# Another order of the instructions up to the first gate and up products, and seven products without use on TensorE in the opening

## The chip, the cores and the metric

The kernel runs on one core of one Trainium2 chip. The metric is the time of one execution on the device in microseconds (us), the median of several runs. The profile is of one further execution. Engines are named as the profile names them: PE (TensorE), DVE (VectorE), ACT (ScalarE), POOL (GpSimd) and SP (SyncE, which here only issues DMAs).

## The reference, cut to what matters

One decoder layer on x of 512 rows by 1024 columns, in float32. In short:

```
h    = rms_norm(x, attn_pre_norm)
proj = h @ w_in                         # one projection for both head groups
A    = 4 heads of differential attention: softmax(q1 k1) - lam * softmax(q2 k2), times v, then rms_norm
B    = 8 heads in 2 groups: g0 * compressed branch + g1 * selected branch + g2 * window branch
x    = x + rms_norm(concat(A, B) @ w_out, attn_post_norm)
f    = (silu(h2 @ w_gate) * (h2 @ w_up)) @ w_down,   h2 = rms_norm(x, ffn_pre_norm)
out  = x + rms_norm(f, ffn_post_norm)
```

The compressed branch passes blocks of 32 keys and values through a small two-layer network (k_cmp_w1, v_cmp_w1 and the like). With 512 rows the selected branch and the window branch reach every earlier row.

## The kernel before, in words

Every operand of a large product is split into a high part (float32 rounded to the form that PE multiplies in one pass) and a low part (the rest); a product is then hi*hi + hi*lo + lo*hi, three matmuls. ACT makes the high parts, DVE (in places POOL) the low parts. Names ending in h and l, or beginning with whi and wlo, are these parts.

The first two thirds of the program's instructions are written as some thirty *streams*, Python generators that issue a few instructions and then yield. Each stream has a letter. `TABLE` is a string of 1543 letters: the program takes them one after another and advances the stream of that letter by one step. So the string fixes the order of the instructions on each engine, and the order on each engine is kept: an instruction whose operands aren't ready holds all behind it on that engine. SP issues its DMAs in the same way, one behind the other. What lies behind the first gate and up products (the feed-forward part, from the products `gw` at L1250 on) is written out and isn't in the table.

The streams that the text speaks of:

- `a` x_loads, `b` x_highs, `c` x_lows: load x transposed in eight parts, scale it and split it into xh and xl. `b` also issues three products `warm` without use, and squares the parts (xraw, in place); `c` adds the squares up.
- `d` constants: the masks and the identity.
- `e` row_factors (L365 on): sums the squares over the partitions on PE with eight small products into ssum, makes the factor rstd of each row on ACT and DVE, spreads it with four products rb, and multiplies the rotation tables (ckv, skv, cos, sin) with it on DVE.
- `S` weights: loads 512 KB parts of the weights into wraw (three buffers), and splits them (three buffers for whi, three for wlo).
- `P` projections (L432 on): the products of the input projection in the order C v1 q1 k1 cv n1 ck s g q0 k0 v0 n0. The first pair, C (tiles fm4 and fm5), is multiplied in the order of the list OPEN as the parts of x come in. cv and ck are the first layer of the small network (tile cmp), n1, s and so on are pairs of tiles fm. The tiles fm, v and cmp take turns in two buffers of PSUM.
- `R` evictions: reads the fm tiles (ACT copies fm4 and fm5 to craw), rotates them on DVE into rope, splits them and writes them to memory (kcvc, qk).
- `K` compression: reads kcvc back as cx and makes cst, the operand of cmp, on ACT and DVE.
- `Q` loads: reads the queries and keys back (qst, kst). `A` scores: products sc. `X`, `E`, `Y`: row maximum on DVE, exponential on ACT, scaling of the rows (for the heads N the first of four row blocks on ACT, the other three on POOL). `Z`, `H`, `L`: transposes tr on PE and their split into pth and ptl. `V`: products av. `O`, `J`: outputs and their split into oh and ol (with the products ms and rsb for the norm of the heads D).
- `G`, `T`: the compressed scores scc, and their transposes trc.
- `W`, `M`, `N`: the output weights and the products mixp, mix. `w` to `z`: the norms of the four row blocks, with the transposes trh. `F`: the first gate and up products gu.

The heads are taken in the order D2 D3 N4 N5 N6 N7 D0 D1 N0 N1 N2 N3. The products without use multiply xh with itself into a PSUM tile (warm_ps) that nothing reads; before, 20 of them on zeros stand ahead of everything, and three on xh behind the first two parts of x.

Of the kernel before, what the change touches and what calls it, by code (L numbers as in the profile page):

```python
# [17 lines left out]
P = 128  # L18
# [30 lines left out]
HEADS = "D2 D3 N4 N5 N6 N7 D0 D1 N0 N1 N2 N3"  # L49
WORDER = "2 3 6 7 0 1 F0 4 5 F1"  # L50
TABLE = (
    "aaabbcaabbaaPcbPbcbaPaPbaaPbabcPPPPaaccPcPbPbPPPbPPbPcbPPcPdPbdcdPbPPcPbcPSPbcPcPPPPcPPPPcedPPPSSSSeePeP"
    "ePPPPaaPdSeeeRePPeRRSSRRRPRPPPSRPRSRPRSPPPSRRPKPRPPPPRSRPPRPSPSSSaKKPPPPPPPRRSPPPPPSSPSRRRRSSPPPPPRRdRKK"
    "KSRRSKSdPKPKRRRPSPQSdSPSPSSPRSPSPPKSRKKKKKdSRPPSPKKRPdSRdKKPPSRRRSSSdSPPPKdRKKKKKKKPPQSPRRSSKRPSPPPSSPAA"
    "SXPSQEXRRPSRPASPPQRKKPRPPSPSSXXARSARQXPPSEAPXRPKPQKESXGSPRPEESPKSKRPRAdAXPRSSKXdXEKESPRGRRRRPAPPEXGPRRPE"
    "RYRPPPPPRYYYXGPRRPPRGRYPYEYYYPPGSGSPSPPQRPQGGGEZQZQPHPLASAQERXXZAEQHXXARGGSSSSRPEEPERXSYPPGEAXXEGPAPAGYA"
    "HLGXVPRYAELXVREPEXYPSAGEVPVXEOXOYPGXSREPAPERRYRYRPSJJXJYSTPTYZSRRYXTJRPATAPHXZPSLYREJEZPQPAYPRESRJHPSHLX"
    "SRRRRRPJXPAEYYVYPLXZZRPREAPWRXXHRRYJEHVLXPPEEYAZRVHVSRXPWOPQAPOYYPYYWLRSZLHPYWSVLAEYXZXHLZAXWXVPAVRHYXPL"
    "VZYARHYXLEPPPRWVZVHZLPEPTAHESXTRAPVEPEEYVEXWAQVZHYPLWERZPXWPLROHWLWAYEJOWJZWJVPPJYQHXWVYYXLPVXRRAXTVVWYQ"
    "QRWYYVVEEEVTVRZAOHZAEAOJXHLRXLZYEJYHRMZJQARJHEELVMYVVYQRLXVEXYZHYXMRXZAALEEYYQVVHXVZLMAQHLVUZVZYXEJHXYJX"  # L60
    "AHELXALMEZOAAZUHXYHOXXLLYAMYGYVYVZGEVYYYHVGVYGMXLEEUWWEGVXZHZGVGEVLQVHGMOZMQEGHOGMEALLJEJXXAGAVXGEQUEYEY"
    "AQXMGXEGAYVXXEGGWVVMOMEAMGUOWYWGATXAXTJTMYYYYXEMTAJJYEZXJUHZAHWYMMXEALJEWWXLZMYYYYYYYYQXMEZEAJEXHLVWVHZJ"
    "MAXHALEEWVEVLZXWOYYMZOHQAYYXXELHEXAVYVLWXYYYJJEVZEVAAHXJEJEZLVXVHXVZLAJVEEVZMXOAHMXOHLEYLYWJWZZAJXAVHHLE"
    "ELXXYVTTZVYHYYJVXVZAWYLXVAWYWWMMEYHEEZLMHZEHXMLVVTEJYTWLVYOMWZZHYMOLVVJYYYHYZJWVVHLYLVZHMWLVYYZZVVVHHLML"
    "OZOHZLHMVVLZWWWVZHVLHLVVWVVVWOWOMOJOMMJJMMMMJBBBBNBNNNBwwwwwNxNxxwxxwxxxwwwxwwWNwNNNNxWNxwNxxwxwwNxwwxxx"
    "xxwwwNxNxxNxNWWWWNNNyWWyNyNNzyyzFFyyzFyzyFFzzzzyyyFFyzyzyFzyWzzzzyWFyyzzyyFzzzyyyzFzzFz"
)
HP = 400
POOL_LO = "157"
# [48 lines left out]
def hybrid_block_kernel(  # L118
# [6 lines left out]
    act, dve, pool, pe, sp = nc.scalar, nc.vector, nc.gpsimd, nc.tensor, nc.sync  # L125
# [81 lines left out]
    def ps(tag, name, dt=F32):  # L207
        return PS.tile([P, SEQ], dt, tag=tag, name=name, bufs=PSB[tag])
# [6 lines left out]
    warm_ps = ps("av", "warm")  # L215
# [24 lines left out]
    act, dve, pool, pe, sp = (Written(e) for e in (act, dve, pool, pe, sp))  # L240
    xh, xl = [], []
# [121 lines left out]
    def row_factors():  # L363

        yield ["sums", "ident"]  # L365
        ssum = ps("tr", "ssum")[:, :NT]
        for i in range(NT):
            for j in range(2):
                pe.matmul(ssum[:, i:i + 1], obj["sq", j][:, i * P:(i + 1) * P], ones, start=(j == 0), stop=(j == 1))
        yield  # L370
        v, y, t = (cpool.tile([P, NT], F32, tag=f"rr{j}h", name="rr", bufs=2) for j in range(3))
        act.activation(y, ssum, AF.Ln, bias=eps, scale=1.0 / D_MODEL)
        act.activation(y, y, AF.Exp, scale=-0.5)
        yield
        dve.tensor_scalar(v, ssum, 1.0 / D_MODEL, EPS, OP.mult, OP.add)
        yield
        dve.tensor_tensor(t, y, y, OP.mult)
        dve.tensor_tensor(t, t, v, OP.mult)
        dve.tensor_scalar(t, t, -0.5, 1.5, OP.mult, OP.add)
        dve.tensor_tensor(rstd, y, t, OP.mult)  # L380
        yield
        rb = ps("tr", "rb")
        for i in range(NT):
            pe.matmul(rb[:, i * P:(i + 1) * P], rstd[:, i:i + 1].to_broadcast([P, P]), ident, start=True, stop=True)
        yield
        dve.tensor_scalar_mul(nrstd, rstd, -1.0)
        for j in (2, 3, 0, 1):
            yield ("rope", j)
            dve.tensor_tensor(rp[j], rb, rp[j], OP.mult)
            obj["table", j] = True  # L390
# [43 lines left out]
    def projections():  # L434
        for tok in PROJ.split():
            if tok == PROJ.split()[0]:
                ms, pts, done = [2 * PAIR[tok] + j for j in range(2)], [], [0, 0]
                for j, k, part in OPEN:
                    m = ms[j]
                    yield [("w", m)] + [[("xh", k)], [("xh", k), ("wl", m)], [("xl", k)]][part]  # L440
                    if not done[j]:
                        pts.append(ps("mm", f"fm{m}"))
                    w = obj["w", m][int(part == 1)]
                    pe.matmul(pts[j], w[:, k * P:(k + 1) * P], (xh, xh, xl)[part][k], start=(done[j] == 0),
                              stop=(done[j] == 3 * NK - 1))
                    done[j] += 1
                    if done[j] == 3 * NK:
                        del obj["w", m]
                        obj["fm", m] = pts[j]
            elif tok in PAIR:  # L450
                for m in (2 * PAIR[tok], 2 * PAIR[tok] + 1):
                    yield ("w", m)
                    hi, lo = obj.pop(("w", m))
                    pt = ps("mm", f"fm{m}")
                    for n in range(3 * NK):
                        if n and n % 4 == 0:
                            yield ("wl", m) if n == NK else None
                        w, x_ = ((hi, xh), (lo, xh), (hi, xl))[n // NK]
                        k = n % NK
                        pe.matmul(pt, w[:, k * P:(k + 1) * P], x_[k], start=(n == 0), stop=(n == 3 * NK - 1))  # L460
                    obj["fm", m] = pt
            elif tok[0] == "c":
                v = int(tok == "cv")
                for c in range(4):
                    yield [("w", tok, c), ("xs", v, c // 2)]
                    if not c:
                        hps = ps(CMPT, f"cmp{v}")
                    hl = obj.pop(("w", tok, c))
                    for l in range(4):
                        if l == 2:  # L470
                            yield
                        lh = 4 * c + l
                        t = obj["xs", v, lh // 8][:, lh % 8].rearrange("p s g n -> p (s g n)")
                        for wi, w in enumerate(hl):
                            pe.matmul(hps[:, :CMP_HIDDEN], t, w[:, l * 256:(l + 1) * 256],
                                      start=(lh == 0 and wi == 0), stop=(lh == NLH - 1 and wi == 1))
                obj["cmp", v] = hps
            else:
                cs, width = (2, 256) if tok[0] == "v" else (3, NVG)
                kc = NK // 2 if cs == 2 else 3  # L480
                ws = []
                for i in range(NT):
                    n = 0
                    for c in range(cs):
                        yield None if i else ("w", tok, c)
                        if not n:
                            pt = ps("mm", tok)[:, :width]
                        if not i:
                            ws.append(obj.pop(("w", tok, c)))
                        for j, (xx, wi) in enumerate(((xh, 0), (xl, 0), (xh, 1))):  # L490
                            if j == 2:
                                yield
                            for k in range(kc * c, min(kc * (c + 1), NK)):
                                w = ws[c][wi][:, (k - kc * c) * width:(k - kc * c + 1) * width]
                                pe.matmul(pt, xx[k][:, i * P:(i + 1) * P], w, start=(n == 0), stop=(n == 3 * NK - 1))
                                n += 1
                    obj[tok, i] = pt
# [668 lines left out]
    act, dve, pool, pe, sp = nc.scalar, nc.vector, nc.gpsimd, nc.tensor, nc.sync  # L1166
# [418 lines left out]
    for n, (r, c, t) in enumerate(banks):  # L1585
        i, bank = 2 * r + t, result[r][c][t]
# [7 lines left out]
        m, v, y, e, f, _, s0, s1 = (rows[i][:, j:j + 1] for j in range(8))  # L1594
# [106 lines left out]
```

## Time and profile before

| | us |
|---|---|
| median of 3 runs | 654.77 (654.54, 654.77, 657.61) |
| the profiled execution | 658.55 |
| its span in the profile | 656.5 |
| PE busy in the span | 636.7 (97%) |
| DVE busy | 545.3 (83%) |
| mean clock granted to TensorE | 0.991 |

The profile is a page and a trace that can be asked. Its timeline has a start, a duration, the engine, and for merged rows the number of instructions behind an x; brackets hold the idle time before and what ended it. The durations of matmuls overlap, so the pace of a run of them is the distance of the starts. A small float32 product (ssum, rb, ms, rsb) stands as two records. PEclk in a table of windows is the clock that TensorE was granted, 1.00 for the full one.

### The profile page before, as it was taken

The numbers are of one execution on the slowest core, as the hardware profiler recorded it, in microseconds if no ns is written. First come the engines' busy times: TensorE is split into PE (matmuls) and PEld (weight loads), VectorE is DVE, ScalarE is ACT, GpSimd is POOL, SyncE is SP. The second block draws the span as 40 slices with busy tenths as digits, with TensorE's granted clock in tenths as the row PEclk, the third lists the DMA queues.
The fourth block names the chain that finished last, engine by engine and source line by source line (L and its number), as shares of the span: only waits on it lengthen the run. The fifth ranks groups of instructions, "written<-read, shape, count | busy, mean of one in ns | idle before, by whom it ended". The sixth has DMA issues, their size and how long they took to land.

```text
span 656.5 us, 11115 instructions
## 1 busy us (share of the span) xinstructions
PE 636.7 (97%) x4081; PEld 569.9 (87%) x4081; DVE 545.3 (83%) x1050; ACT 390.6 (59%) x821; POOL 94.4 (14%) x100
## 2 busy tenths in 40 slices
PE   9899899999999999999999999999999999999995
PEld 5788789788988888887898999999999998888884
DVE  5757887789789798978999998888888639999866
ACT  7334554575567688955756655655655539675434
POOL 0000001112316236532200000000000101120023
PEclk9799999999999899999999999999999999999999
DMA  8354796715315423145414333223223547984543
GB/s 307 124 162 185 251 309 231 237 36 202 136 35 206 137 106 113 65 178 205 163 34 142 115 103 123 97 97 129 97 97 129 127 131 203 307 257 132 199 90 128
DMA packets 32902, 100.52 MB, mean 153 GB/s; under 512 B 4176, under 2 KB 5072, under 8 KB 31952
## 3 DMA queue, kind: packets, MB, share of 16 engines
q1 hardware_dynamic: 30544, 95.62, 41.8%
q0 software_dynamic: 2304, 4.20, 3.8%
q8 instruction: 32, 0.52, 0.3%
q14 instruction: 22, 0.18, 0.1%
HBM read 85.64 MB, written 12.06 MB: 149 GB/s over the span
## 4 chain that ended last, share of the span: by engine, by line
PE 77%; DVE 12%; DMA 4%; ACT 3%; issue 2%; SPq 0%; DVEq 0%; ACTq 0%
PE gw L1250 28%; PE acc L1461 17%; PE fm L230 9%; PE av L230 4%; PE v L230 4%; PE sc L230 3%; PE mix L230 3%; PE tr L230 3%; PE g L230 2%; DMA wraw<-in_wf 2%; PE scc L230 1%; DVE rr L230 1%; DMA qk<-rope 1%; DVE mixt L230 1%; PE mixp L230 1%
## 5 line engine op out<-in xcount | busy, mean ns | idle before, releaser
L230 POOL TENSOR_TENSOR p<-p,l 128x384 f32<-128x384 f32 (+3 forms) x60 | 54.5, 939 | 126.0 <-DVE l L230 101.3
L230 ACT ACTIVATE p<-p,nm 128x128 f32<-128x128 f32 (+1 forms) x96 | 53.2, 556 | 12.3 <-DVE nm L230 10.3
L230 DVE CUSTOM_DVE_ANT_0 p<-sc,mask_b 128x128 f32<-128x128 f32 (+1 forms) x96 | 44.6, 483 | 7.1 <-PE sc L230 5.5
L230 ACT ACTIVATE whi<-wraw 128x1024 fp32r<-128x1024 f32 (+2 forms) x34 | 34.9, 1034 | 24.3 <-issue 13.1
L230 DVE TENSOR_TENSOR wlo<-wraw,whi 128x1024 fp32r<-128x1024 f32 (+2 forms) x34 | 40.9, 1209 | 8.6 <-ACT whi L230 8.6
L230 ACT ACTIVATE pth<-tr 128x384 fp32r<-128x384 f32 (+1 forms) x60 | 30.7, 521 | 25.1 <-PE tr L230 22.6
L230 DVE TENSOR_TENSOR ptl<-tr,pth 128x384 fp32r<-128x384 f32 (+1 forms) x60 | 35.2, 595 | 10.4 <-ACT pth L230 10.2
L230 PE MATMUL sc<-kst,qst 128*128 128x128 f32 (+1 forms) x192 | 41.3, 331 | 2.2 <-DMA kst<-qk 1.5
L1396 POOL DMA_DIRECT2D dr<-in_wd x8 | 7.0, 880 | 235.8 <-DVE wu L1284 189.3
L230 PE MATMUL fm<-xh,whi 128*128 128x512 f32 x128 | 35.4, 403 | 0.5 <-ACT whi L230 0.5
L230 PE MATMUL fm<-xh,wlo 128*128 128x512 f32 x128 | 35.0, 401 | 0.0
L230 PE MATMUL fm<-xl,whi 128*128 128x512 f32 x128 | 33.7, 394 | 0.0
L230 PEld LDWEIGHTS sc<-kst,qst 128*128 128x128 f32 x192 | 28.8, 189 | 5.3 <-DVE vn L230 1.9
L230 PE MATMUL tr<-ident,p 128*128 128x128 f32 x200 | 31.4, 280 | 1.4 <-DVE ptl L230 1.3
L230 PE MATMUL mix<-ws,oh 128*128 128x512 f32 x84 | 29.6, 403 | 0.0
L230 PEld LDWEIGHTS tr<-ident,p 128*128 128x128 f32 x200 | 24.2, 144 | 5.6 <-DVE ptl L230 1.8
L230 PEld LDWEIGHTS fm<-xl,whi 128*128 128x128 f32 x128 | 24.2, 190 | 5.0
L230 PEld LDWEIGHTS fm<-xh,wlo 128*128 128x128 f32 x128 | 24.1, 192 | 4.9
L230 PEld LDWEIGHTS fm<-xh,whi 128*128 128x128 f32 x128 | 23.5, 192 | 5.0 <-ACT whi L230 1.0
L1461 PE MATMUL acc<-whi,ah 128*128 128x512 f32 x60 | 23.5, 392 | 0.0
L1461 PE MATMUL acc<-whi,al 128*128 128x512 f32 x60 | 23.5, 392 | 0.0
L1461 PE MATMUL acc<-wlo,ah 128*128 128x512 f32 x60 | 23.5, 392 | 0.0
(368 smaller groups left out, 1956.0 us busy)
## 6 DMA issues: line engine op xcount, KB each, us to landing
wraw<-in_wg SPq DMA_DIRECT2D x22, 512.0 KB, 3.3
dr<-in_wd SPq DMA_DIRECT2D x22, 512.0 KB, 4.5
wu<-in_wu SPq DMA_DIRECT2D x19, 512.0 KB, 3.2
wraw<-in_wf SPq DMA_DIRECT2D x16, 512.0 KB, 4.7
qk<-rope SPq DMA_DIRECT2D x7, 1024.0 KB, 4.9
qst<-qk SPq DMA_DIRECT2D x24, 256.0 KB, 2.7
kst<-qk SPq DMA_DIRECT2D x24, 256.0 KB, 4.1
wraw<-in_wo SPq DMA_DIRECT2D x8, 512.0 KB, 3.3
```

Of the source, the lines that this page charges most:

```text
L230: r = getattr(self.eng, name)(*a, **k)
L1250: m = pe.matmul(pt, ww[:, k * P:(k + 1) * P], hx[k], start=(start and n == 0), stop=(n == 11), skip_group_check=True)
L1396: pool.dma_start(t[:, H], wd[pair(p)[0]][:, L], accum_op=OP.add)
L1461: m = pe.matmul(pt, x, y, start=(start and n == 0), stop=(stop and n == 2), skip_group_check=True)
```

## The change

The string TABLE is another one of the same length: each letter occurs as often as before, in another order throughout. And two streams issue more products without use: row_factors two, behind the first of the eight products ssum, and projections five, behind the last product of C. The core of the diff (of the table one line of fifteen):

```
 TABLE = (
-    "aaabbcaabbaaPcbPbcbaPaPbaaPbabcPPPPaaccPcPbPbPPPbPPbPcbPPcPdPbdcdPbPPcPbcPSPbcPcPPPPcPPPPcedPPPSSSSeePeP"
...
+    "aaaabbbcPcPaPPcaabbPaPaPcbPPPbacPPacPbPPPaPPPPbbPPbcPSPPPbPcbaPPPPPPPPabbcdbbaPSSdabcccbPScccceePPPPSSeP"
...
@@ row_factors
                 pe.matmul(ssum[:, i:i + 1], obj["sq", j][:, i * P:(i + 1) * P], ones, start=(j == 0), stop=(j == 1))
+                if i == j == 0:
+                    for _ in range(2):
+                        pe.matmul(warm_ps, xh[0][:, :P], xh[0], start=True, stop=True)
@@ projections, behind the loop over OPEN
+                for _ in range(5):
+                    pe.matmul(warm_ps, xh[0][:, :P], xh[0], start=True, stop=True)
```

What the order of the instructions makes of it is shown at three places.

**First place: PE in the opening.** Before, from the last part but one of x on:

```order
L230 MATMUL fm4_148<-xh6_177,whi_133 128x512
L230 MATMUL ssum_249<-ones_85,xraw_127 128x1 x8
L230 MATMUL fm5_181<-xh6_177,whi_152 128x512
...
L230 MATMUL rb_283<-ident_78,rstd_87 128x128 x4
...
L230 MATMUL fm5_181<-xl7_220,whi_152 128x512
L230 MATMUL v1_306<-whi_267,xh0_131 128x256
```

The same stretch after:

```order
L230 MATMUL fm4_140<-xh6_198,whi_134 128x512
L230 MATMUL ssum_257<-ones_85,xraw_127 128x1
L230 MATMUL warm_100<-xh0_132 128x512 x2
L230 MATMUL ssum_257<-ones_85,xraw_127 128x1 x7
L230 MATMUL fm5_165<-xh6_198,whi_157 128x512
...
L230 MATMUL rb_286<-ident_78,rstd_87 128x128 x4
...
L230 MATMUL fm5_165<-xl7_244,whi_157 128x512
L230 MATMUL warm_100<-xh0_132 128x512 x5
L230 MATMUL v1_321<-whi_250,xh0_132 128x256
```

Two products stand between the first and the second ssum, five between the last product of C and the first of v1; five products fm stand between ssum and rb, and six behind rb, in both. The three products on xh that were ahead of fm4 stand behind its fourth product now, and on DVE the casts of the masks have moved from ahead of the row factors to behind the first row blocks of v1.

**Second place: DVE and SP around the second product cmp** (cmp0, of ck; it takes the PSUM buffer of fm14 and reads cst). DVE before, where wlo_745 is the low part of ck's second weight part:

```order
L230 SCALAR_TENSOR_TENSOR rope_764<-fm14_683,cos_122 128x512
L230 TENSOR_TENSOR cst_762<-cx_716,cst_762 128x8x2x31
L230 TENSOR_TENSOR cst_762<-pos_718,cst_762 128x8x2
L230 TENSOR_TENSOR cst_770<-cx_716,cst_770 128x8x2x31
L230 TENSOR_TENSOR wlo_745<-wraw_680,whi_744 128x1024
L230 SCALAR_TENSOR_TENSOR rope_764<-fm14_683,sin_123 128x512
```

DVE after, where the same low part is wlo_761:

```order
L230 SCALAR_TENSOR_TENSOR rope_777<-fm14_677,cos_122 128x512
L230 SCALAR_TENSOR_TENSOR rope_777<-fm14_677,sin_123 128x512
L230 TENSOR_TENSOR wlo_761<-wraw_675,whi_760 128x1024
L230 TENSOR_TENSOR cst_783<-cx_718,cst_783 128x8x2x31
L230 TENSOR_TENSOR cst_783<-pos_720,cst_783 128x8x2
```

fm14 is read to the end, and ck's second weight part split, ahead of the cst instructions and no longer behind them. SP before, where in_wf are the two weight parts of the pair s, the next that PE multiplies:

```order
L230 DMA qk4_735<-rope_603 128x2048
L230 DMA wraw_741<-in_kw1 128x1x1024
L230 DMA kst_782<-qk4_735 64x1024 x2
L230 DMA wraw_792<-in_wf 128x1024
L230 DMA wraw_817<-in_wf 128x1024
```

SP after:

```order
L230 DMA wraw_756<-in_kw1 128x1x1024
L230 DMA qk4_775<-rope_584 128x2048
L230 DMA wraw_787<-in_wf 128x1024
L230 DMA kst_799<-qk4_775 64x1024 x2
L230 DMA wraw_813<-in_wf 128x1024
```

The first part of s is asked for ahead of the two reads kst, which wait for the write qk4 to land, and no longer behind them. On PE the first six products sc, which stood inside cmp0, are behind it.

**Third place: PE at the first scores of head N4** (kst_1248 before, kst_1249 after). Before:

```order
L230 MATMUL sc_1289<-kst_1219,qst_1211 128x512 x2
L230 MATMUL sc_1302<-kst_1248,qst_1242 128x128 x2
L230 MATMUL sc_1302<-kst_1248,qst_1242 128x256 x2
L230 MATMUL fm0_1214<-xh4_167,wlo_1199 128x512
...
L230 MATMUL fm1_1342<-xh3_160,whi_1310 128x512
```

After:

```order
L230 MATMUL sc_1294<-kst_1230,qst_1226 128x512 x2
L230 MATMUL fm0_1253<-xl0_142,whi_1214 128x512
...
L230 MATMUL fm0_1253<-xl7_244,whi_1214 128x512
L230 MATMUL fm1_1315<-xh0_132,whi_1279 128x512
...
L230 MATMUL fm1_1315<-xh7_202,whi_1279 128x512
```

N4's scores followed those of D3 at once; now eight products of fm0, eight of fm1 and three transposes stand between them. The two DMAs that fetch kst stand at the same place of SP's order, right behind the qst of N4.

Two more counts from the order on PE. Between the second and the third group of transposes of N4 stood four products fm and the four rsb; now four fm, rsb, four trc, eight v0 and two sc. And between the last score of N3, the last head, and its first transpose stood 21 products mix, 20 transposes, 17 av and 4 trc; now 12 mix, 16 transposes, 13 av and 4 trc. From the last product of the second mix0 tile to the first trh are 45 products mix before and 42 after.

More of the change, by code (lines that the diff above doesn't have):

```diff
@@ L51 @@
 TABLE = (
-    "aaabbcaabbaaPcbPbcbaPaPbaaPbabcPPPPaaccPcPbPbPPPbPPbPcbPPcPdPbdcdPbPPcPbcPSPbcPcPPPPcPPPPcedPPPSSSSeePeP"
[L53 to L66, printed above, removed]
+    "aaaabbbcPcPaPPcaabbPaPaPcbPPPbacPPacPbPPPaPPPPbbPPbcPSPPPbPcbaPPPPPPPPabbcdbbaPSSdabcccbPScccceePPPPSSeP"
@@ new lines @@
+    "eeePPPPPPeeRSeeRRRaSRPPRPPPPPRRPRRRKPPSSPRdRddSPPPSRRPSPPSPRPPSSPRKPPRPRKPPPKSSSPdPPSSPRRPKRPSSSPRPKKRdR"
+    "RRRRKSPSSKRPPPPSPQRPSSSSPPPPPPdSSKSKKSPRPKPKdKSKRKSKPRKPSSSPPPdRRPSRRSPPPRRRSKKKKSKdKKRSRQPSPKSSKSQdPPSP"
+    "PPPSSSASAXEAXPQRPRKSSPPPKPRdKKPQPXARSRASdPXRXAQRSGSXEXREKPPARXPXPEKSEEASEEKdPASRSRPRPXKPPPPRRYRPGGPYRRRP"
+    "RPRRXPPGEPYYRRRPPPPEPPGYPGGYGRRYSYRSYZGQGQZQPHPSQGPESPXHRRLRPRSPAAAXSPPQXPSPESESRZXGHEXAVSPRXEEGPGYYAXPL"
+    "LXEVSPSAAPXPPYGYARRXYXEXGVVRPAEQOAROYASEJGEPRPXPERYYGPEEXTRXJJYSXRAZSRAHESPEPPSJLTZPEJYXHXSTRRRYPYRXEYAT"
@@ new lines @@
+    "ZPEAJYQLPPRREHJPZLARXVHXLVZPVYSPZRRWRRYHRYXXYAELRPXHEVAZOOYAYREPLPPZHVEVYXVRAAVHYPRLYYZEELPVPYTSQHXJTSPV"
+    "EXXWPWLZZHXRPWWEAPQEPHRXASLVXLVVPYZPYOEXYPAHRLOEZQEAEHAXXYWZPPLPHXZWWPWWWWEERRPLYPYYJWHLVYVVVVRTRARVVXVW"
+    "JRVRTZAJYAERJXRZOHOAJLYXEXYWHEZMQLQHJALRZQJEJZVHQEYYYYXHLXVVXMJMRZYAMHYEXVYLXVEAAZELZWUXYWAVVHYAXVLXEZEV"
+    "MHLXQQAXHEZLEAAOHWJZYXLXEOMZGGVYVVWHLYGUYYYYVHYGYEEWUVVEVXGZLGVEGQVZGXWEHLEMYMZQOOHJYGLGYMGAGXHAVLQVAVQG"
+    "VXGOGMAWMEYXOJYXUAXGMXAEEGYXQGYJTAEXJEEAXXMYAMTXYEETTJJEWAEZAYJXHEZHLYMYYLMYAXZYJWUEXZYAHUHXVWLQVLEZMAVW"
@@ L67 @@
+    "YJXXEZHXVEYEALJHMAXWOOEXWWWLAAYYZYVEYHJVEVJWYMVXMLZWJJEYVYHMWELXZHMELXZHVEVAXELYZXMZVVYAYHHELOXLZATAOEHX"
+    "LYJXAYZYMTEJYXHZELVJXVZVEVVHVVJXAWLEZVVYMYWHEMXHOLETLZYMYYOTHZVYYYYYYVLZHVVVHLJLZHMYZVVLZVWHHVOLYLZMZWJO"
+    "HMHVLLVZZWWWWVHHVLVVLWVVVMOOOOMMMWJJJWJWMBBBBMMBMMNMBWWWwwNwwNNNwNxwwxxxxxxwxNNNwwxwwNxwWxwNxxxxwNwNwwNx"
+    "xxxxNNWNNwWwwxwxxxNNNNNyyyzyWyyzNyyFFzzzyzFFzFFyWFzWyyzFyyFzyyzzzyzyyyzFzzzzzFyFyyzyzzz"
 )
```

## The prediction

> **What bounds the kernel now.** I read the page first: PE is busy 97% of the span, and 77% of the chain that ended last is PE's.
>
> ```profile
> span 656.5 us, 11115 instructions
> PE 636.7 (97%) x4081; PEld 569.9 (87%) x4081; DVE 545.3 (83%) x1050; ACT 390.6 (59%) x821; POOL 94.4 (14%) x100
> PEclk9799999999999899999999999999999999999999
> PE 77%; DVE 12%; DMA 4%; ACT 3%; issue 2%; SPq 0%; DVEq 0%; ACTq 0%
> ```
>
> The change adds PE work and takes none away, so it can only gain where PE waits or runs below full speed. The clock row names two such places: the second slice at 0.7 and the fourteenth at 0.8. Next I asked what PE waits for from 60 to 360 us, the stretch whose order is new (columns: total, times, longest):
>
> ```profile
> PE trh L230 <- DVE mixt L230: 1.7, 4, 0.5
> PE cmp L230 <- DVE rope L230: 1.6, 1, 1.6
> PE sc L230 <- DMA kst<-qk: 1.5, 1, 1.5
> PE tr L230 <- DVE ptl L230: 1.3, 1, 1.3
> PE fm L230 <- ACT whi L230: 0.5, 1, 0.5
> ```
>
> Three of these are single waits above 1 us. So the sum has five terms: the opening, three waits, and the close of the attention part.
>
> **The opening.** The windows ahead of 30 us give the clock (column before the last two), and the timeline the pace:
>
> ```profile
> 16.31:19.72 3.41, 2.05 (x13) 1.48 (x12) 3.41 (x8) 2.12 (x4) 0.00 (x0) 1.00 0.77 304
> 19.72:23.13 3.41, 3.41 (x14) 3.02 (x14) 1.59 (x8) 0.47 (x2) 0.00 (x0) 0.50 0.45 154
> 23.13:26.55 3.42, 3.42 (x14) 3.03 (x13) 1.11 (x2) 0.00 (x0) 0.00 (x0) 0.50 0.02 5
> 26.55:29.96 3.41, 2.96 (x21) 2.48 (x20) 3.41 (x6) 2.78 (x4) 0.00 (x0) 1.00 0.01 2
> ```
>
> ```profile
> 16.78 0.39 PE L230 MATMUL fm<-xh,whi 128*128 128x512 f32 x1
> 18.31 0.38 PE L230 MATMUL ssum<-ones,xraw 128*128 128x1 f32 x2 [1.14 <-DVE xraw L230]
> 18.92 2.44 PE L230 MATMUL ssum<-ones,xraw 128*128 128x1 f32 x14 [0.22 <-DVE xraw L230]
> 21.22 0.77 PE L230 MATMUL fm<-xh,whi 128*128 128x512 f32 x1
> 23.50 1.91 PE L230 MATMUL rb<-ident,rstd 128*128 128x128 f32 x8
> 25.06 1.20 PE L230 MATMUL fm<-xh,whi 128*128 128x512 f32 x2
> 27.83 0.74 PE L230 MATMUL v<-whi,xh 128*128 128x256 f32 x4 [0.45 <-ACT craw L230]
> ...
> 39.62 2.00 PE L230 MATMUL fm<-xh,whi 128*128 128x512 f32 x8
> 41.46 1.98 PE L230 MATMUL fm<-xh,wlo 128*128 128x512 f32 x8
> ```
>
> ```profile
> 22.52 0.16 DVE L230 TENSOR_TENSOR rstd<-rr 128x4 f32<-128x4 f32 x1
> ```
>
> ```profile
> 142.94 0.80 PE ms L230 x8
> 245.04 0.89 PE rsb L230 x8
> ```
>
> PE waits 1.14 us for the sums of the squares, then streams one column per product; at 19.72 us the clock falls to 0.50 and stays there for two windows, 6.83 us. At full clock an fm takes 0.23 (eight from 39.62 to 41.46), a record of ssum 0.10 (as ms) and one of rb 0.11 (as rsb). So the 14 records of ssum would take 1.4 and not the 2.3 up to 21.22; the five fm 1.15 and not 2.28; rb 0.9 and not 1.56; the six fm 1.4 and not the 2.3 from 25.06 to the wait ahead of v. That is 3.6 us, and half of 6.83, 3.4, is all that the clock can hide. rstd is made at 22.68, 1.3 us behind the last ssum, so some 0.2 of that would show behind the five faster fm. An opening at full clock is worth 3.2 us.
>
> The products cost: two at 0.23 in the 0.22 that PE waits there anyway, +0.2; five at 0.23, 1.15, against the 0.45 for craw, which v needs for its PSUM buffer, +0.7. At half clock they cost twice: 0.9 - 0.2 and 2.3 - 0.45, +2.5. Bounds: -3.2 + 0.9 = -2.3 if the clock never falls, +2.5 if it falls as before, +0.9 where it didn't fall without them either. The two products fill 0.45 us of a thin stretch of some 3 us (17.2 to 20.5), too little to call it busy; but the clock moves in whole windows, and I take that one of the two is saved: 3.41 at half speed, -1.7, +0.9: **-0.8 us**. All behind on PE moves with it: the products v and the two pairs fm follow without a wait of PE. The moved three products on xh cost nothing, since the parts of x set the pace there; the casts of the masks leave DVE's way ahead of the row factors, some 0.1 us.
>
> One page speaks against the fall itself. The Trainium skill, "TensorE: Matmul & The Clock Gate", section "HAM oscillation — how this bites in real kernels", gives as the abstract rule that PE stays at full clock without idle gaps over some 3.4 us. By that rule a wait of 1.14 us would not halve the clock, the products would buy nothing, and the term would be the +0.9 above. The row at 19.72 shows the fall, and the row decides.
>
> **The second product cmp.** DVE, SP, ACT and PE around 80 us:
>
> ```profile
> 78.82 1.23 DVE L230 TENSOR_TENSOR wlo<-wraw,whi 128x1024 fp32r<-128x1024 f32 x1
> 79.95 1.29 DVE L230 SCALAR_TENSOR_TENSOR rope<-fm,sin 128x512 f32<-128x512 f32 x2
> 80.80 0.35 PE L230 MATMUL cmp<-whi,cst 128*128 128x256 f32 x1 [1.60 <-DVE rope L230]
> 80.00 1.12 SPq L230 DMA_DIRECT2D kst<-qk  x2
> 81.24 2.20 SPq L230 DMA_DIRECT2D wraw<-in_wf  x2
> 86.03 1.06 ACT L230 ACTIVATE whi<-wraw 128x1024 fp32r<-128x1024 f32 x1 [0.78 <-DMA wraw<-in_wf]
> 87.14 2.09 PE L230 MATMUL fm<-xh,whi 128*128 128x512 f32 x8 [0.53 <-ACT whi L230]
> ```
>
> cmp0 waits 1.60 us for the PSUM buffer of fm14, whose last reader on DVE stands behind three cst and a wlo. In the new order that reader stands ahead of them, so cst is what is late next: by 1.3 us of moved work, and DVE had been idle ahead of cst. Then PE waits 0.53 for the pair s: its load could be asked for only at 81.24, behind the two kst and behind the low part that ends at 80.05 and frees a buffer; both have moved, so the load can start ahead of the 80.00 at which kst is issued. Together 2.1. Within cmp0 the third and fourth weight parts still follow each other at 1.23 on DVE, while PE needs less than a microsecond for each, so a few tenths come back: **-1.9 us**, bounds -2.1 and 0. DVE's order and SP's hold here: behind qk4 only kst waits for its landing.
>
> **The first scores of N4.** The chain there:
>
> ```profile
> 119.54 4.90 DMA kst<-qk
> 124.58 0.70 PE sc L230 x4
> ```
>
> PE waits 1.5 us for kst. Sixteen fm at 0.23 and three transposes, 4 us, now stand ahead, more than the wait; kst keeps its place in SP's queue: **-1.5 us**, bounds -1.5 and 0.
>
> **The third transposes of N4.**
>
> ```profile
> 149.57 1.05 PE L230 MATMUL rsb<-ident,rs 128*128 128x128 f32 x8
> 151.97 0.55 PE L230 MATMUL tr<-ident,p 128*128 128x128 f32 x3 [1.35 <-DVE ptl L230]
> ```
>
> The trc, eight v0 and two sc put between are, at 0.11 for each trc and 0.12 for each v0 (96 from 27.83 to 39.62) and 0.23 for each sc, about 1.9 us more cover for a wait of 1.35. DVE's own order there is new too, so ptl may come later: **-0.9 us**, bounds -1.35 and +1.35.
>
> **The close.** The last scores (of N3), POOL's scaling of them, and their first transposes:
>
> ```profile
> 269.38 0.62 PE L230 MATMUL sc<-kst,qst 128*128 128x512 f32 x2
> 275.13 2.65 POOL L230 TENSOR_TENSOR p<-p,l 128x256 f32<-128x256 f32 x3 [5.14 <-ACT pct L230]
> 280.29 0.92 PE L230 MATMUL tr<-ident,p 128*128 128x128 f32 x7
> ```
>
> From 269.84 to 280.29 PE worked 10.45 us. Nine mix (0.23, as fm), four tr (0.11, as rsb) and four av (0.18, an estimate between these two) fewer leave 10.45 - 2.1 - 0.4 - 0.7 = 7.3. POOL had finished at 277.78, 7.9 us behind the scores, so at the old pace PE waits 0.6. At trh, the first wait of the list, three mix fewer are 0.7 less cover. **+1.3 us**, bounds 0 and +3.8 (the full 10.45 and the 0.7).
>
> All else in the new order I cost at nothing. It could remove the rest of the listed waits or make as many, and PE and DVE work are equal but for the seven products. Behind 324 us nothing is added; a gain ahead of it passes on, because the chain from the last mix on starts from PE.
>
> **The sum.** -0.8 - 1.9 - 1.5 - 0.9 + 1.3 = -3.8 us. Against the profiled execution, 658.55 with a span of 656.5, that is 654.75; against the median 654.77, **651.0**. The profiled execution is 3.8 us above that median, and 657.61 stands among the three runs: stretches at half clock that not all executions have would do that, each costing 1.7.
>
> **The rivals.**
>
> 1. *The clock term is nothing.* If the median run had no half clock in the opening, or one that the products don't end, the term is +0.9 and not -0.8: 652.7. For it: the 3.8 us between profile and median. Against: the thin stretch is there in every execution. In a sentence of its own: the Trainium skill, same page, section "What's actually happening", has the window free-running, so that where it lies in the thin stretch differs from execution to execution; the trace agrees on its length, two windows of 3.41.
> 2. *Both windows saved*: the term is -2.3: 649.5. For it: the two products stand in the very wait. Against: 0.45 us of work in a window of 3.41.
> 3. *The waits come back elsewhere.* An order that fills one gap takes the filler from another; if the terms from 60 us on add to nothing, -0.8 remains: 654.0. For it: the close above. Against: the removed waits stand at places where nothing took their cover.
> 4. *Slower: thin stretches at half clock.* The opening falls as before and the products run at half clock, +2.5; and the close, now thinner, waits its full 3.8 and loses one window, 1.7, as PE did from 221.1 us on:
>
> ```profile
> 221.10:224.52 3.42, 3.42 (x16) 3.12 (x14) 1.16 (x3) 1.36 (x4) 1.21 (x1) 0.50 0.32 77
> ```
>
> With -4.3 for the three waits that is +3.7: 658.5. It decides from the point at which POOL ends over 9 us behind the last scores and the window of the second ssum is thin all the same.
>
> **How the numbers follow.** 0.5% of the median, 3.3 us, is about what a measurement of this kernel can tell from no change: below 651.5 is faster, above 658.0 slower. The forecast, 651.0, has 0.46; its own range is 649.5 to 652.5, so 0.33 of that lies under faster and 0.13 under same. Rival 1 has 0.18 (0.03 faster, 0.15 same), rival 2 0.13 (faster), rival 3 0.12 (same), rival 4 0.11 (0.10 slower, 0.01 same). That is faster 0.49, same 0.41, slower 0.10. The range takes in rival 2 with the transposes at their bound and the close at nothing (648), and rival 3 with the opening at +0.9 (655.7); rival 4 is left out.
>
> **What would show it.** Right: the windows between 16 and 27 us with at most one at 0.50, v starting by 27.1; no wait of cmp for rope and of fm for whi near 80 us; no wait of sc for kst near 120; the first gw some 4 us before its 359 us. Wrong: v starting after 28 us; a new single wait of over 1.5 us between 130 and 300 us in the list of waits, most of all before N3's transposes; or two runs of the same kernel further apart than the change.

## The result, and the profile after

The changed kernel takes **651.33 us** (median of 11 runs, 649.04 to 653.43) beside 654.96 for the kernel before (median of 11): a ratio of 0.9933, 95% interval 0.9915 to 0.9951, so a gain of 0.5 to 0.9%. The forecast was 651.0 in a range of 648.0 to 655.7. The profiled execution took 651.21 with a span of 649.3, so it is an ordinary one; that of before, 658.55, was 3.6 above its own median. Of the 7.2 us between the two spans only half is the change. One execution of the experiments below, the profiled one of e1_table, took 1595 us; it is left out of every figure, and e1 has no profile to read.

Three lines of the page of the changed kernel, which answer to those of before:

```profile
span 649.3 us, 11142 instructions
PE 633.5 (98%) x4088; PEld 569.0 (88%) x4088; DVE 542.5 (84%) x1050; ACT 390.8 (60%) x821; POOL 90.2 (14%) x100
PEclk9899999999999999999999999999999999999998
```

PE is the bound as before, and is busy for 98% and not 97%. The row of the clock has an 8 in its second slice, where before had a 7 there and an 8 at 221 us: the opening with one slow window for two, and nothing at 221. The 8 of the last slice lies behind the last product, which starts at 642.00.

The four longest waits of PE between 60 and 360 us (total, times, longest) of the changed kernel:

```profile
PE trh L230 <- DVE mixt L230: 1.5, 1, 1.5
PE tr L230 <- DVE ptl L230: 1.0, 1, 1.0
PE cmp L230 <- DVE cst L230: 0.8, 1, 0.8
PE sc L230 <- DMA kst<-qk: 0.6, 1, 0.6
...
```

cmp no longer waits for rope. The other names look like the old ones, but they stand elsewhere: this wait for ptl is at 251 us and not at 152, this wait for kst at 83 us and not at 123, and the wait for mixt is one of 1.5 in the place of four of at most 0.5.

The windows of the opening (time, then PE's busy time; the column of the clock is the third from the right) of the changed kernel:

```profile
17.01:20.43 3.42, 2.58 (x19) 2.06 (x18) 3.06 (x5) 1.61 (x3) 0.00 (x0) 1.00 0.54 214
20.43:23.84 3.41, 3.41 (x13) 2.93 (x13) 0.99 (x6) 0.47 (x2) 0.00 (x0) 0.50 0.63 192
23.84:27.25 3.41, 3.41 (x20) 2.96 (x20) 2.67 (x5) 1.51 (x3) 0.00 (x0) 1.00 0.02 5
```

One window at 0.50 where before had two. PE's timeline there, with the two products between the thin ones and the five ahead of v:

```profile
18.39 0.38 PE L230 MATMUL ssum<-ones,xraw 128*128 128x1 f32 x2 [0.84 <-DVE xraw L230]
18.64 0.71 PE L230 MATMUL warm<-xh 128*128 128x512 f32 x2
19.19 1.84 PE L230 MATMUL ssum<-ones,xraw 128*128 128x1 f32 x14
...
25.77 1.30 PE L230 MATMUL warm<-xh 128*128 128x512 f32 x5
26.91 0.64 PE L230 MATMUL v<-whi,xh 128*128 128x256 f32 x4
```

v starts at 26.91 and not at 27.83.

Around the second cmp, DVE's and PE's timeline of the changed kernel:

```profile
78.48 0.70 DVE L230 SCALAR_TENSOR_TENSOR rope<-fm,sin 128x512 f32<-128x512 f32 x1
79.08 0.70 DVE L230 SCALAR_TENSOR_TENSOR rope<-fm,cos 128x512 f32<-128x512 f32 x1
79.67 1.24 DVE L230 TENSOR_TENSOR wlo<-wraw,whi 128x1024 fp32r<-128x1024 f32 x1
80.81 0.20 DVE L230 TENSOR_TENSOR cst<-pos,cst 128x16 fp32r<-128x16 f32 x1
81.06 0.38 PE L230 MATMUL cmp<-whi,cst 128*128 128x256 f32 x1 [0.82 <-DVE cst L230]
83.88 1.52 PE L230 MATMUL sc<-kst,qst 128*128 128x128 f32 x8 [0.60 <-DMA kst<-qk]
```

The wait of 1.60 at the start of cmp is gone; one of 0.82 stands in its middle, and one of 0.60 behind it. The chain of waits there shows what the second hangs on:

```profile
74.01 5.75 DMA qk<-rope
...
80.31 3.44 DMA kst<-qk
...
83.88 1.52 PE sc L230 x8
```

The keys are written to memory and read back, 5.75 and 3.44, together 9.2 us; between the two transfers no instruction of PE or DVE stands in this chain.

At the first scores of N4 and at the third transposes PE has no wait any more (its timeline, changed kernel):

```profile
118.41 1.98 PE L230 MATMUL fm<-xh,wlo 128*128 128x512 f32 x8
120.23 1.44 PE L230 MATMUL sc<-kst,qst 128*128 128x128 f32 x8
...
150.47 0.52 PE L230 MATMUL sc<-kst,qst 128*128 128x384 f32 x2
150.83 0.49 PE L230 MATMUL tr<-ident,p 128*128 128x128 f32 x3
```

### The profile page after: what moved, and what is told of

Its sections match the earlier page's. It is cut to its first block, busy times and chain, and to the rows that moved or that the text cites. A ratio compares the mean times of both kernels' runs of the same rounds, so it can differ in the third digit from the quotient of the medians.

```text
span 649.3 us, 11142 instructions
## 1 busy us (share of the span) xinstructions
PE 633.5 (98%) x4088; PEld 569.0 (88%) x4088; DVE 542.5 (84%) x1050; ACT 390.8 (60%) x821; POOL 90.2 (14%) x100
## 4 chain that ended last, share of the span: by engine, by line
PE 77%; DVE 13%; ACT 4%; DMA 3%; issue 2%; SPq 0%; DVEq 0%; ACTq 0%
PE gw L1256 28%; PE acc L1467 17%; PE fm L230 10%; PE av L230 4%; PE v L230 4%; PE sc L230 4%; PE mix L230 3%; PE tr L230 3%; PE g L230 2%; DVE rr L230 1%; PE scc L230 1%; DVE wlo L230 1%; DVE rope L230 1%; ACT p L230 1%; DVE p L230 1%
## 5 line engine op out<-in xcount | busy, mean ns | idle before, releaser
L230 POOL TENSOR_TENSOR p<-p,l 128x384 f32<-128x384 f32 (+3 forms) x60 | 49.9, 862 | 142.7 <-DVE l L230 109.4
L230 PE MATMUL fm<-xh,whi 128*128 128x512 f32 x128 | 34.1, 398 | 0.0
```

The lines of the kernel that those rows point to most:

```text
L230: r = getattr(self.eng, name)(*a, **k)
```

## The experiments

My theory behind the first four: the order of the table takes away waits of some 3 us behind 60 us, and the products save half a microsecond or more of half clock in the opening. The rivals: the products carry the gain; the products do nothing; the gain comes from places that I had costed at nothing. The runs of a group share the chip and the runs of the kernel before.

| run | median us | before | ratio (95%) | mean clock, before's |
|---|---|---|---|---|
| e1_table | 651.15 | 656.14 | 0.9931 (0.9912 to 0.9950) | 0.9942, 0.9935 |
| e2_products | 656.09 | 656.14 | 0.9995 (0.9979 to 1.0011) | 0.9948, 0.9935 |
| e3_new_to_28 | 655.14 | 656.14 | 0.9988 (0.9968 to 1.0009) | 0.9947, 0.9935 |
| e4_new_to_140 | 653.00 | 656.14 | 0.9949 (0.9931 to 0.9968) | 0.9945, 0.9935 |
| e5_new_to_84 | 654.46 | 657.02 | 0.9968 (0.9946 to 0.9990) | 0.9944, 0.9931 |
| e6_new_to_212 | 652.37 | 657.02 | 0.9921 (0.9893 to 0.9950) | 0.9947, 0.9931 |
| e7_four_ahead | 651.96 | 657.02 | 0.9914 (0.9889 to 0.9939) | 0.9950, 0.9931 |
| e8_two_only | 652.77 | 657.02 | 0.9933 (0.9907 to 0.9959) | 0.9949, 0.9931 |
| e9_changed_again | 652.90 | 656.54 | 0.9940 (0.9918 to 0.9962) | 0.9951, 0.9921 |
| e10_cst_early | 652.16 | 656.54 | 0.9932 (0.9903 to 0.9961) | 0.9958, 0.9921 |
| e11_two_waits_less | 652.03 | 656.54 | 0.9935 (0.9911 to 0.9958) | 0.9967, 0.9921 |
| e12_and_four_ahead | 651.01 | 656.54 | 0.9917 (0.9889 to 0.9944) | 0.9960, 0.9921 |

The mean clock is that of all timed executions of the kernel, the profiled one among them. Where the text says that a figure is on the first chip's count, the ratio has been multiplied by the 654.96 us of the first measurement.

### The table alone

The new string without the seven products:

```
@@ row_factors
-                if i == j == 0:
-                    for _ in range(2):
-                        pe.matmul(warm_ps, xh[0][:, :P], xh[0], start=True, stop=True)
@@ projections
-                for _ in range(5):
-                    pe.matmul(warm_ps, xh[0][:, :P], xh[0], start=True, stop=True)
```

> The new order of the table alone, without the seven products. My theory (the table takes away waits of some 3 us behind 60 us, and the two products save one of two half-clock windows of the opening): both windows between 16 and 27 us are at 0.50 again, v starts near 27.8 us as before, the waits of cmp for rope near 80 us and of the first scores for a 1.5 us kst are gone, and the time is about 652.1 (the changed kernel's 651.3, less 0.9 for the products, plus 1.7 for the window). Rival 1 (the gain is the clock's, from the products): 654 to 655. Rival 2 (the products do nothing but cost their own time): one window at 0.50 here too, v near 26.1, and about 650.4.

Measured 0.9931, where the whole change gives 0.9933. Rival 1 falls: the table carries the gain. The texts count from a kernel before of 654.9, which on this chip takes 1.2 more; the theory's 652.1 is then 653.3, just outside the interval (650.4 to 652.9), and rival 2's 650.4 is 651.6, which is what the ratio gives. The windows and the start of v that the text names can't be read without a profile.

### The products alone

The old string with the seven products:

```
@@ row_factors
+                if i == j == 0:
+                    for _ in range(2):
+                        pe.matmul(warm_ps, xh[0][:, :P], xh[0], start=True, stop=True)
@@ projections
+                for _ in range(5):
+                    pe.matmul(warm_ps, xh[0][:, :P], xh[0], start=True, stop=True)
```

> The old order of the table with the seven products alone. My theory: one window between 16 and 27 us at 0.50 and not two, v near 27.0 us, all the old waits behind 60 us as they were, about 654.1 (654.9 less 0.8). Rival 1 (the gain is the clock's): 651 to 652. Rival 2 (the products do nothing but cost their own time): two windows at 0.50, v near 28.7, about 655.8.

Measured 0.9995, between the theory (0.9988) and rival 2 (1.0014, just outside the interval): no change that can be seen. 1 minus the clock, times the span, is the time lost to half clock (start and end of the execution counted). It is 4.3 us in the mean of before's 23 executions and 3.4 in the 12 with the products: 0.8 saved, but by the spread of the executions that is 0.8 give or take 1.1, and the middle execution of both loses 3.3. So neither the saving nor a cost of the products is clear of nothing. The waits of PE behind 60 us in this profile:

```profile
PE cmp L230 <- DVE rope L230: 1.6, 1, 1.6
PE tr L230 <- DVE ptl L230: 1.4, 1, 1.4
PE sc L230 <- DVE nm L230: 0.8, 1, 0.8
PE sc L230 <- DMA kst<-qk: 0.7, 1, 0.7
```

The waits for rope and ptl are the old ones. The 0.8 stands at N4's first scores (123.19 us): here kst came in time, and PE waited for nm, the row maximum on DVE, instead. So the 1.5 of the profile before had a second releaser close behind (there nm is made at 123.84 and kst lands at 124.44). The 0.7 for kst is at 226.92, at the scores of another head.

### The new order up to a point, the old one behind it

Four places: the letters of the new string up to number n, and then all that are left, in the order of the old one. The seven products are in all of them.

```
-TABLE = new
+TABLE = new[:135] + rest of old          # e3, up to 28 us
+TABLE = new[:335] + rest of old          # e5, up to 84 us
+TABLE = new[:590] + rest of old          # e4, up to 140 us
+TABLE = new[:985] + rest of old          # e6, up to 212 us
```

> The new order up to the first products of v1 (28 us), with the seven products, and the old order behind it. My theory: v near 26.9 us, then the waits of cmp for rope (1.6), of the first scores of N4 for kst (1.5) and of the third transposes for ptl (1.3) again, about 654.1. Rival (the order of the opening carries the gain, since what it shifts on SP, ACT and DVE brings all later loads ahead): those waits are shorter by over a half, and the time is 652.5 or less.

> The new order with the seven products up to some 84 us, behind the second product cmp, and the old order behind it. My theory, as corrected by the first four runs (products nothing, order up to 140 us some 3 us of gain): the place of cmp gives a part only, since cmp now waits 1.0 for cst and the scores behind it 0.8 for kst; the waits of the first scores of N4 (1.5) and of the third transposes (1.3) are back; about 654.5. By the prediction's terms, -1.9 for this place, 653.5. Rival (the two later places carry nothing, the whole gain is made ahead of 84 us): 653 or less, and g starts as early as in the kernel that is new up to 140 us.

> The new order with the seven products up to some 140 us, behind the first scores of N4, and the old order behind it, N3's close included. My theory (the gain is made by the opening and the waits up to 150 us, and the new close gives 1.3 back): the waits near 80 and 120 us are gone or short, mix and trh stand as close as before, and the time is 650 to 652. Rival (the gain comes from the many small waits of 150 to 240 us that I costed at nothing): 653 to 654, with the old waits of scc, mixp and sc between 150 and 240 us in the gaps of PE.

> The new order with the seven products up to some 212 us and the old order behind it, with the old close of N3. By the prediction's term (the new close costs 1.3): about 650.0, with no wait of over 0.7 us from the last transposes of N3 to trh. Rival (behind 212 us the new order gains rather than loses): 652 to 653, since the waits of scores and mixp that stood between 204 and 240 us come back.

The medians fall step by step: 0.9995 (no new order), 0.9988, 0.9968, 0.9949, 0.9921, and 0.9933 and 0.9940 with all of it. In us that is 0.5, 1.3, 1.3, 1.8, and 0.8 to 1.2 back. No step alone is clear of the intervals (each ratio's is 1.1 to 1.9 either way); the way from 28 to 212 us, 4.4, is. So the opening's order carries little (e3's rival falls), and nothing shows a gain behind 212 us.

By the median e5 is no success for its text: 0.9968 is 652.9 on the first chip's count (651.4 to 654.3), which is the rival's 653 and not the theory's 654.5. The profiles tell the places better, though e5's is the slowest of its 12 executions (660.22). In it, new only up to 84 us, the later waits are all there:

```profile
PE sc L230 <- DMA kst<-qk: 4.3, 3, 1.9
...
PE tr L230 <- DVE ptl L230: 1.3, 1, 1.3
...
PE cmp L230 <- DVE cst L230: 0.9, 1, 0.9
```

Of the 4.3, 1.9 stand at the first scores of N4 and 1.5 behind the second cmp. So PE still loses at the two later places, against the rival; how much they carry in the median e5 doesn't tell. The rival's other sign decides nothing: g starts 72.2 us behind v in e5 and 71.9 in e4. In e4 the waits at N4 and for ptl are gone, while those at the second cmp (0.87) and behind it (1.16) remain. Its 0.9949 is 0.6 to 1.0 us above what the whole string gives; on a chip that takes 1.2 more, 653.0 is inside the theory's range (651 to 653, shifted) and below the rival's (654 to 655), whose lower end lies just outside the interval (651.6 to 654.0). e6, at 0.9921, is 649.8 on the first chip's count (648.0 to 651.7): the prediction's case, 650.0, and not the rival's 652 to 653. Yet its profile shows what the rival named as well; the list of waits of e6 between 200 and 325 us:

```profile
PE sc L230 <- DMA kst<-qk: 1.7, 2, 1.1
PE trh L230 <- DVE mixt L230: 1.4, 3, 0.5
...
```

The scores wait again, 1.7 in all, and trh waits 1.4 in three pieces where the changed kernel has one of 1.5. But waits of scores for kst stand here in other profiles of the changed kernel too (e9: 0.71 at 198.78 and 1.36 at 224.27), so they say nothing of the order behind 212 us. The two closes are of nearly the same make, and e7, with the new close and on the same chip as e6, has 0.9914.

The rows of the clock of e3 and e5 show something else that the texts left out:

```profile
PEclk9999999899999999999999999999999999999998
PEclk9799999899999999999999999999999999999999
```

In both, the 8 in the eighth slice is a window at half clock behind the wait for kst at N4 (1.86 us up to 123.13 in e3, 1.93 up to 126.13 in e5; the clock falls at 124.6 and 126.4). These are the two longest waits of any profile; behind those of up to 1.6 us the clock did not fall outside the opening. Of the four profiles with the old order at N4, three have a window at half clock between 28 and 640 us (these two and the 221 us of before), of the nine with the new order none.

### Other products

In the place of the seven, four ahead of the first ssum; and the two without the five:

```
@@ row_factors, e7
+        for _ in range(4):
+            pe.matmul(warm_ps, xh[0][:, :P], xh[0], start=True, stop=True)
         for i in range(NT):
@@ projections, e7 and e8
-                for _ in range(5):
-                    pe.matmul(warm_ps, xh[0][:, :P], xh[0], start=True, stop=True)
```

> The new order; in the place of the seven products, four stand ahead of the first ssum, where PE waits some 0.9 to 1.3 us for the squares. If the products cost only where nothing hides them: at the full clock the time is that of the order without products (some 0.8 less than with the seven), the clock loses as little as with the seven or less, and the median is about 650.5. Rival (the half clock comes from the one-column products and not from the wait): the clock loses as much as without products, 651.3.

> The new order with the two products between the first ssum and without the five. If the two are what raises the clock of the window: the time at the full clock is 0.6 less than with the seven, the clock loses the same (3.0 us in the mean), about 650.7. Rival (the five are what helps, since they keep the window behind rb full): the clock loses as much as without products (3.8), 651.5.

All three forms lose 3.0 to 3.4 us to half clock (the changed kernel 3.0, e7 3.3, e8 3.4, before beside the last two 4.5), and their ratios, 0.9933, 0.9914 and 0.9933, can't be told apart. Nor can the clock of any from that of e1 without products (3.8), as each of these means is good to 1 us or so. e7's interval takes in its theory (650.5, a ratio of 0.9933) and just leaves out the rival (651.3, 0.9945); e8's takes in both of its own. The profile of e7 shows what the place does:

```profile
17.43 1.07 PE L230 MATMUL warm<-xh 128*128 128x512 f32 x4
18.63 0.38 PE L230 MATMUL ssum<-ones,xraw 128*128 128x1 f32 x2
19.23 1.72 PE L230 MATMUL ssum<-ones,xraw 128*128 128x1 f32 x14 [0.22 <-DVE xraw L230]
...
25.36 0.74 PE L230 MATMUL v<-whi,xh 128*128 128x256 f32 x4 [0.45 <-ACT craw L230]
```

The wait for the first squares (0.84 us in the changed kernel, 1.14 before) is filled; the 0.22 for the next is left. v starts at 25.36 in this profile without half clock in the opening, and at 25.88 and 25.89 in the two such profiles with the seven: the four cost 0.5 less. And without the five, v waits 0.45 us for ACT, as it did before, so that much of the five's 1.1 us (of five starts at the pace of 0.23) is hidden too.

### What cmp waits for

In the changed kernel, the last part of cst made ahead of what stood before it (two letters K moved up):

```
-SKKKKSKdKKRSRQPSPKSSKSQdPP
+SKKKKSKdKKKKRSRQPSPSSSQdPP
```

> The changed kernel once more, as the measure for the three kernels beside it: 0.993 of the kernel before, some 651.3 to 652.8 as the chip goes. If the stretch from v to the first gw takes 324.9 us in this profile too, the figures of the first profile are the kernel's; if it takes over 327, the place by place comparison of single profiles holds to some 2 us only, as the waits for kst (0.3 to 1.5 behind the second product cmp in the runs so far) would let expect.

> The changed kernel with one change at the second product cmp: the last, small part of cst is made on ACT ahead of the weight part that waits for a buffer there, and on DVE ahead of two rope and a wlo. If cst is the cause of cmp's 0.8 us wait, as the releaser named says (theory 1), the wait is gone and cmp ends 0.8 earlier. If the low part of the third weight part is as late (theory 2: it ends at 80.81 us where cst ends at 81.0, since its high part waits on ACT for a buffer that fm frees at 78.2), the wait stays at 0.6 to 0.8 with wlo as the releaser, and the time is the same. Either way the wait of the scores for kst behind it takes what is won, since that load is issued at 79.8 us by SP and stays there.

PE's timeline of e10 at that place, one row:

```profile
82.83 0.38 PE L230 MATMUL cmp<-wlo,cst 128*128 128x256 f32 x1 [0.74 <-DVE wlo L230]
```

Theory 2: the wait is 0.74 and names wlo. The releaser named in the changed kernel was merely the later of two: there wlo ends at 80.91 and cst at 81.01. The medians, 652.16 and e9's 652.90, can't be told apart. That the wait for kst behind cmp takes the rest was wrong for this profile, which lists none there. It changes from execution to execution: the same two transfers in e9,

```profile
74.51 6.05 DMA qk<-rope
...
81.11 4.02 DMA kst<-qk
85.27 1.52 PE sc L230 x8
```

and in e12, where SP's and DVE's order there is the same:

```profile
72.73 5.30 DMA qk<-rope
...
78.58 3.52 DMA kst<-qk
82.24 1.52 PE sc L230 x8
```

6.05 and 4.02 against 5.30 and 3.52: 1.3 us, and PE waits 1.5 in the one and 0.2 in the other. From v to the first gw(hth,wh) e9 took 326.7 us, the first profile of the same kernel 324.9. That is short of the 327 of e9's second case, but it says the same: single profiles compare to some 2 us only. The two profiles of the old string, before and e2, have 331.3 and 328.0 there.

### Two waits less

In the changed kernel, a step F (eight gu) ahead of the last transposes, and DVE's wlo behind the ptl for which PE waits at 251 us; in e12 also the four products ahead of ssum in the place of the seven:

```
-VYHMWELXZHMELXZH ... zyzyyyzFzzzzzFyFyyzyzzz
+VYHMELWXZHMELXZH ... zyzyyyzFzzFzzzyFyyzyzzz
```

> The changed kernel with two letters of the table moved: a step of the gu products ahead of the last transposes trh, where PE waits 1.5 us for mixt, and on DVE a wlo behind the ptl for which PE waits 1.0 us at 251 us. If a wait ahead of the first gw that is filled or shortened passes on to the end, as the prediction says: 0.95 and 0.6 less, about 1.5 us below the changed kernel beside it, first gw 1.5 closer to v. Rival (the work behind is bound by something else, such as ACT and DVE making hth and htl, or the loads): less than 0.5 lower, with a wait for hth, htl or cy in its place.

> The kernel with the two letters moved, and four products ahead of the first ssum in the place of the seven. If the four cost nothing, being in a wait, and keep the clock as the seven do: 0.7 less at the full clock than with the seven, so about 2.2 us below the changed kernel, 0.990 of the kernel before. Rival (their place does not matter): as the kernel with the two letters moved.

The timeline of PE and ACT in e11:

```profile
316.35 1.29 PE L230 MATMUL trh<-ident,mixt 128*128 128x128 f32 x8 [0.54 <-DVE mixt L230]
...
344.07 0.63 ACT L1277 ACTIVATE t4h<-t 128x512 fp32r<-128x512 f32 x1 [4.01 <-DVE t L1291]
...
346.60 0.36 ACT L1304 ACTIVATE cy<-gw 128x256 f32<-128x256 f32 x1
...
347.01 1.20 PE L1256 MATMUL gw<-rope,whi 128*128 128x256 f32 x8 [1.36 <-ACT cy L1304]
```

The waits fell as written, from 1.48 to 0.54 and from 1.1 to 0.4. But 30 us later PE waits 1.36 for cy, which stands on ACT behind a t4h that waits for DVE. The first profile of the changed kernel has that t4h at 344.77 and no wait at this place: counted from v (25.89 here, 26.91 there) the t4h is no earlier in e11, 318.2 and 317.9. At the first gw product of all e11 is 0.8 closer to v than the first profile (315.1 and 315.9), at gw(hth,wh) 1.3 farther (326.2 and 324.9). In e12 the wait for cy is 0.8. The medians are 652.03 and 651.01 beside 652.90: 0.9 and 1.9 lower, with intervals that overlap. The rival for e11, given back at a wait for cy, is what the profile shows; the median alone can't separate 0.5 from 1.5. e12 has the lowest median of its group, but isn't shown to beat the changed kernel.

## Why the prediction was right, step by step

The total, 651.0, came out within 0.3 us, and the table's order is what carries the gain, as the prediction has it. But the sum's terms were off both ways, and that they cancel to 0.3 us is luck.

- **The opening, -0.8.** Forecast: one of two windows saved, -1.7, and +0.9 for the products. The profile shows one window and v 0.92 earlier, as written. But it is a draw of the lot: the nine profiles with the seven products have no half clock in the opening (v at 25.88 and 25.89), one window (v between 26.91 and 27.74, five profiles) or two (28.82 and 29.00). Over the timed executions of e2 the saving is half the forecast's, 0.8, and not clear of nothing, and the products alone move the median by -0.05%, within -0.21 and +0.11. The mis-sized step is that one window saved in one profile was counted as a window saved in the median. In us e2's interval is -1.4 to +0.7, so the forecast's -0.8 lies inside it and the +0.9 of rival 1 ("the clock term is nothing") just outside. In a sentence beside it: the Trainium skill, "TensorE: Matmul & The Clock Gate", section "What's actually happening", has the window free-running, and the trace agrees as far as the windows lie elsewhere in each profile: the one that holds the first ssum begins at 17.01 in the changed kernel and at 18.00 in e9.
- **The second cmp, -1.9.** In the first profile it brought about -0.7: by the distance of PE's starts, less the usual pace, 1.76 and 0.70 us lost there became 0.98 and 0.76. Over all profiles it is less: the listed waits at the start of cmp, in it or behind it and for whi are 1.0 to 2.4 us, 1.75 in the mean, in nine profiles with the new order there (e10 apart), and 1.8 to 2.1, 1.94 in the mean, in three with the old. So this term was worth some 0.2. The step that failed is "a few tenths come back": the low part of the third weight part ends at 80.91 and comes no earlier when cst does (e10), and the scores behind cmp wait 0.2 to 1.5 us for kst in those nine profiles, where with the old order they don't wait. The prediction did not ask when the write ahead of the reads kst is issued: counted from v that is 47.1 to 47.6 us in the first profile, e9 and e12, against 45.2 to 46.1 in before, e2 and e3. And the second read then takes 3.4 to 4.0 us, against 3.0 in before and e2. Whether the load of s, which now stands ahead of the reads, slows them was not tried. That the wait for whi would go was right: PE's next fm follow the scores without one.
- **The first scores of N4, -1.5**, and **the third transposes, -0.9.** Both waits are gone in every profile with the new order there, and stand in all that have the old one (0.8 to 1.9, the 0.8 for nm in e2, and 1.3 to 1.4). By the distance of PE's starts, less the pace of such products, before lost 1.63 and 1.51 us there, the changed kernel nothing. The cover was enough and ptl came no later, so the second term was 0.6 too small.
- **The close, +1.3.** Its mechanism did not come: no wait of PE is listed between 264 and 300 us, so POOL's scaling was not late, and at trh the single wait for mixt, 1.5, with one of 0.4 for rr, is about what the four were, 1.7. What the new order pays in this stretch is the wait for ptl at 251 us, 1.0, which the text didn't see. Whether the close costs anything in the sum stays open: e6, with the old one, is 0.8 to 1.2 us below the changed kernel by the ratios, within the intervals, and e7 with the new one no higher than e6.
- **All else, 0.** By the listed waits, and with nothing for the products, the terms come to 0 - 0.2 - 1.5 - 1.4 and 1.0 back at 251 us, -2.1 us; the measurement is -3.6. So some 1.5 us lies where the prediction costed nothing, or where no wait is listed. A part of it can be the windows at half clock behind 28 us, 1.7 each, which three of four profiles with the old order at N4 have and none of nine with the new one; so few profiles don't show their share, and it stays open. e4 to e6 had 1.8 between 140 and 212 us, with an interval on each of over 1.2.
- **"A gain ahead of it passes on."** True for gains up to 212 us, as far as the medians show. Not for one made at trh in e11's profile, which gave it back at cy, behind a chain of DVE and ACT that came no earlier; e11's median keeps 0.9 of the 1.5, with an interval that takes in both.
- **The profiled execution.** That windows at half clock lift it above the median is only part of it. It lost 5.9 us by its clock of 0.991 and its span, where the 23 executions beside e1 lost 4.3 in the mean and 3.3 in the middle; that is 1.6 to 2.6 of the 3.6 us that it lies above the median. The rest isn't shown.

Of the signs for right, v at 26.91 and one window at 0.50 came, and the waits for rope, for whi and at N4 for kst are gone. What the prediction calls the first gw, at 359.08, is the first gw(hth,wh); it starts at 351.80, 7.3 us earlier and not 4, against a profile that was itself 3.6 us above its median. Of the signs for wrong, a new single wait of over 1.5 us between 130 and 300 did not come; the largest is 1.04. But two runs of the same kernel do lie further apart than the change, 649.04 and 653.43, 4.4 us against 3.6, and v starts after 28 us in two other profiles with the seven products (28.82 and 29.00). What carries the result is the ratio of the medians, whose interval is clear of 1.

## What to carry to other kernels

When an order is moved, cost each wait by the second releaser, not by the one named: where two end within a microsecond, taking the first away is worth only the difference (here cst and wlo, 0.1 apart). A wait that a DMA round trip ends (here 9 us, different by 1.3 between two executions) is removed for good only by cover longer than its late case. And a gain in the clock seen in one profile is a draw: average the granted clock over all timed executions, and look at the spread of that mean, before counting it.

## What the runs showed of the hardware that was not expected

Whether the clock falls isn't told by PE's busy time in a window. e3's windows around ssum,

```profile
15.31:18.73 3.42, 2.37 (x12) 1.68 (x10) 3.42 (x7) 3.42 (x7) 0.00 (x0) 1.00 1.03 414
18.73:22.14 3.41, 3.41 (x23) 2.85 (x23) 2.17 (x7) 0.62 (x3) 0.00 (x0) 1.00 0.32 117
```

have one of 2.37 us busy that no half clock followed: the wait lay in one window and the thin products (few columns each) in the next. In e10 both lay in one, 2.44 us busy, and two windows at 0.50 followed:

```profile
17.07:20.49 3.42, 2.44 (x17) 1.89 (x15) 3.42 (x5) 2.01 (x4) 0.00 (x0) 1.00 0.57 229
20.49:23.90 3.41, 3.41 (x13) 3.02 (x13) 1.05 (x7) 0.47 (x2) 0.00 (x0) 0.50 0.59 189
23.90:27.32 3.42, 3.42 (x13) 3.03 (x13) 1.36 (x3) 0.00 (x0) 0.00 (x0) 0.50 0.03 8
```

The changed kernel's window began 0.06 us earlier, at 17.01, and had one. What decides between one and two was not tried. And the fall of the kernel before at 221.10 us has a window ahead of it that the profile calls busy throughout:

```profile
217.69:221.10 3.41, 3.41 (x25) 2.99 (x24) 3.38 (x10) 2.76 (x8) 0.07 (x1) 1.00 0.35 122
```

In its 3.41 us stand some fourteen of the products scc, of 32 columns each; that it is again the thin products is a guess that no run here tests. Beside it in a sentence of its own: by the rule of the Trainium skill that the prediction weighed ("TensorE: Matmul & The Clock Gate", section "HAM oscillation — how this bites in real kernels": no idle gaps over some 3.4 us), none of these should have fallen, since no gap in or ahead of them reaches 1.5 us; the rows disagree, as they did before.
